# A blockwise triangular inversion whose updates take half of the columns

## Chip, cores and metric

The kernel runs on one core of a Trainium2 chip. The metric is the time of one execution on the device in microseconds (us): a median of runs. The profile is of one further execution.

## What is computed

One step of a decoder trunk with two layers: 2048 prompt tokens (four tiles of 512) and 8 sequences of 8 decode tokens, model width 1024. The first layer mixes tokens with a gated DeltaNet of six heads, the second with a short convolution; beside each runs a cross-attention into 256 memory tokens, and an output projection follows. What matters here is one step of the DeltaNet. For each head and each chunk of tokens a unit lower triangular system is solved:

```python
    decay = jnp.exp(jnp.where(tril, G[..., :, None] - G[..., None, :], -jnp.inf))
    kb = k * beta[..., None]
    A = jnp.tril(jnp.einsum('bnhid,bnhjd->bnhij', kb, k) * decay, -1)
    rhs = jnp.concatenate([kb * jnp.exp(G)[..., None], v * beta[..., None]], axis=-1)
    wu = lax.linalg.triangular_solve(A + jnp.eye(C, dtype=A.dtype), rhs, left_side=True,
                                     lower=True, unit_diagonal=True)
```

The kernel takes chunks of 128 tokens instead of 64 (the result is the same in exact arithmetic) and inverts the 128x128 matrix of each chunk. The decode tokens are one matrix of 64x64 with eight blocks of 8.

## The kernel before

**Order.** All engines follow one order that is fixed when the kernel is built. A planner (class Flow) runs generators as jobs with priorities and keeps a clock for each engine; each operation moves these clocks by a cost. The matmul helper mm prices a matmul of n fp16 columns at 3 + max(n, 64)/2.4 ns, an ACTIVATE from PSUM is priced at 52 ns + 0.83 ns for each element of a partition, and hops between engines have prices too. A job yields when it waits for another engine, and the planner then takes the job of the best priority that is ready by its clocks. The instructions come out in this order on every engine's queue, and on SP's for the DMAs.

**Work.** In the first layer a loop over heads and token tiles (head_tile) emits the projections of k, q, v and the gate: 24 fp16 matmuls of 512 columns each, weights and activations being split into a high and a low fp16 part. They fill PE while the jobs of the DeltaNet run beside them: wy_decay, wy_k, wy_q and wy_v prepare a head tile of four chunks, two jobs wy_inv invert its matrices (two chunks each), and scan goes through the chunks in order. There are 48 wy_inv for prompt tiles and 6 for the decode tile.

**The inversion** (wy_inv) keeps two fp16 matrices per chunk: U (upper triangular) and L (lower triangular, its transpose), both halves of one tile UL with four blocks of 128 columns: U of the two chunks, then L of the two chunks. Both hold the inverse of the diagonal blocks of the matrix, at first blocks of two. Level li = 1 to 6 goes from blocks of s = 2^li to blocks of 2s (1 to 2 in the decode tile):

1. PE: pq = A16^T L, one matmul of 128 columns per chunk.
2. DVE: qq = pq times a mask. The mask holds the scaled identity and the lower left quarter of each block of 2s, so qq is the identity plus the new quarter.
3. PE: pu = qq^T U and U^T qq, two matmuls of 128 columns per chunk, into four blocks of one PSUM bank.
4. ACT: one ACTIVATE copies the bank (512 columns, fp32) to the fp16 tile UL.

Step 1 of the next level reads L, step 3 reads U. After the last level one correction (tiles pe, ee, u1) follows, and scan waits for its result. The bank is a credit that is given back (gc_.put) after step 4, and qq's buffer (kqc.put) after step 3.

The profile names tiles without numbers: pu is the bank of step 3, ul the tile UL. All matmuls have line L330 (helper mm), all operations of ACT, DVE and POOL line L281 (the helper that keeps the clocks).

Of the kernel before, what the change touches and what calls it, by code (L numbers as in the profile page):

```python
# [15 lines left out]
AF = mybir.ActivationFunctionType  # L16
# [270 lines left out]
def hybrid_kernel(  # L287
# [26 lines left out]
    A = Eng(fl, "ACT", nc.scalar, in_psum)  # L314
# [4 lines left out]
    def mm(out, lhsT, rhs, start=True, stop=True):  # L319
        n = 1  # L320
        for s in rhs.shape[1:]:
            n *= s
        k = lhsT.shape[0]
        if rhs.dtype in (F16, BF16):
            c = 3.0 + max(n, 64) / (2.4 if k == P else 4.8)
        else:
            c = 10.0 + max(n, 128) / 0.6
        fl.op("PE", c if k == rows_in[0] else c + 100.0, out, (lhsT, rhs))
        rows_in[0] = k
        nc.tensor.matmul(out, lhsT=lhsT, rhs=rhs, start=start, stop=stop)  # L330
# [19 lines left out]
    def wait(*flags):  # L350
        for f in flags:
            if not f.on or f.t + HOP > fl.cur.t:
                yield f
# [33 lines left out]
    def psum(tag, shape, bufs, name):  # L387
        t = pp.tile(shape, F32, tag=tag, name=name, bufs=bufs)
        psum_names.add(t.tensor.name)
        return t  # L390
# [4 lines left out]
    def gbank(name):  # L395
        return psum("bank", [P, 4, P], 8, name)
# [10 lines left out]
    def k1(name, dt=F32):  # L407
        return gp.tile([P, 2, P], dt, tag="k1", name=name, bufs=NK1)
# [4 lines left out]
    def kq16(name):  # L413
        return gp.tile([P, 2, P], F16, tag="kq", name=name, bufs=NKQ)
# [985 lines left out]
    def rows(x, n, C):  # L1400
        return x[:n, :n].rearrange("p (o f) -> p o f", o=1).to_broadcast([n, C, n])
# [150 lines left out]
    def wy_inv(it, i):  # L1552

        n, hc = it.n, it.hc
        lv = 7 if n == P else 3
        yield from wait(it.M_ok[i])
        M = it.M[i]  # L1560
        G.tensor_tensor(M[:n, :hc, :n], M[:n, :hc, :n], rows(identKh, n, hc), op=ALU.add)
        yield
        yield from ulc.get()
        yield from kqc.get(2)
        A16 = kq16("A16")
        V.tensor_copy(A16[:n, :hc, :n], M[:n, :hc, :n])
        UL = gp.tile([P, 4, P], F16, tag="k1", name="ul", bufs=NK1)
        U, L = UL[:n, 0:2], UL[:n, 2:4]
        yield
        yield from gc_.get()  # L1570
        pq = gbank("pq")
        for z in range(hc):
            mm(pq[:n, z, :n], A16[:n, z, :n], identh[:n, :n])
        t = fl.cur.t
        G.tensor_tensor(U[:, :hc, :n], A16[:n, :hc, :n], rows(mask_u, n, hc), op=ALU.mult)
        fl.cur.t, fl.cur.eng = t, "PE"
        yield
        V.tensor_tensor(L[:, :hc, :n], pq[:n, :hc, :n], rows(masks[:, 0], n, hc), op=ALU.mult)
        gc_.put()
        yield  # L1580
        Ml = None
        for li in range(1, lv):
            yield from gc_.get()
            pq = gbank("pq")
            for z in range(hc):
                mm(pq[:n, z, :n], A16[:n, z, :n], L[:, z, :n])
            if Ml is None:
                t = fl.cur.t
                Ml = kq16("Ml")
                G.tensor_tensor(Ml[:n, :hc, :n], M[:n, :hc, :n], A16[:n, :hc, :n], op=ALU.subtract)  # L1590
                fl.cur.t, fl.cur.eng = t, "PE"
                Mc.put()
            yield
            yield from kqc.get()
            qq = kq16("qq")
            V.tensor_tensor(qq[:n, :hc, :n], pq[:n, :hc, :n], rows(masks[:, li], n, hc), op=ALU.mult)
            gc_.put()
            yield
            yield from gc_.get()
            pu = gbank("pu")  # L1600
            for z in range(hc):
                mm(pu[:n, z, :n], qq[:n, z, :n], U[:, z, :n])
            for z in range(hc):
                mm(pu[:n, 2 + z, :n], U[:, z, :n], qq[:n, z, :n])
            kqc.put()
            yield
            if hc == 2:
                A.activation(UL[:n, :, :n], pu[:n, :, :n], AF.Copy)
            else:
                A.activation(UL[:n, 0:4:2, :n], pu[:n, 0:4:2, :n], AF.Copy)  # L1610
            gc_.put()
            yield
        yield from gc_.get()
        pe = gbank("pe")
        for z in range(hc):
            mm(pe[:n, z, :n], A16[:n, z, :n], L[:, z, :n], start=True, stop=False)
            mm(pe[:n, z, :n], Ml[:n, z, :n], L[:, z, :n], start=False, stop=True)
        yield
        kqc.put(2)
        yield from kqc.get()  # L1620
        ee = kq16("ee")
        V.tensor_tensor(ee[:n, :hc, :n], rows(identKh, n, hc), pe[:n, :hc, :n], op=ALU.subtract)
        gc_.put()
        yield
        yield from uc.get()
        yield from gc_.get()
        pu = gbank("pu1")
        for z in range(hc):
            mm(pu[:n, z, :n], ee[:n, z, :n], U[:, z, :n])
        kqc.put()  # L1630
        yield
        it.u[i] = k1("u1")
        V.scalar_tensor_tensor(it.u[i][:n, :hc, :n], pu[:n, :hc, :n], 1.0 / MS, U[:, :hc, :n], op0=ALU.mult, op1=ALU.add)
        gc_.put()
        ulc.put()
        fl.set(it.u_ok[i])
# [170 lines left out]
    def head_tile(hd, t):  # L1807
# [13 lines left out]
        for i, (blk, w, dst) in enumerate(((6 + h, wk, kt_), (h, wq, qt_), (12 + h, wv, v_))):  # L1821
# [23 lines left out]
            if i == 0:  # L1845
                fl.spawn(3, chain(start, wy_decay(it)), "decay")
                fl.spawn(3, chain(start, wy_k(it, dn[0])), "wy_k")
                for z in range(it.nh):
                    fl.spawn(1, wy_inv(it, z), f"inv{z}")
            elif i == 1:  # L1850
                fl.spawn(3, chain(start, wy_q(it, dn[1])), "wy_q")
            else:
                fl.spawn(3, chain(start, wy_v(it, dn[2])), "wy_v")
# [449 lines left out]
```

## Time and profile before

| | us |
|---|---|
| median of 3 runs | 2224.36 |
| lowest, highest | 2221.85, 2230.78 |
| profiled execution | 2225.13 |
| its span (first to last instruction) | 2223.4 |
| from the first to the last update matmul of the inversion | 129.2 to 1050.6 |

The span is read as three parts. Up to about 130 us inputs are loaded and normed. Up to about 1056 us the first layer's projections run with the DeltaNet beside them. After that come the first layer's attention and output projection and then the second layer, in which nothing is inverted. Engines: PE is TensorE's matmul, PEld its weight load, DVE VectorE, ACT ScalarE, POOL GpSimd. The rows are in a section of their own below.

### The profile page before, as it was taken

The numbers are of one execution on the slowest core, as the hardware profiler recorded it, in microseconds if no ns is written. First come the engines' busy times: TensorE is split into PE (matmuls) and PEld (weight loads), VectorE is DVE, ScalarE is ACT, GpSimd is POOL, SyncE is SP. The second block draws the span as 40 slices with busy tenths as digits, with TensorE's granted clock in tenths as the row PEclk, the third lists the DMA queues.
The fourth block names the chain that finished last, engine by engine and source line by source line (L and its number), as shares of the span: only waits on it lengthen the run. The fifth ranks groups of instructions, "written<-read, shape, count | busy, mean of one in ns | idle before, by whom it ended". The sixth has DMA issues, their size and how long they took to land.

```text
span 2223.4 us, 43011 instructions
## 1 busy us (share of the span) xinstructions
PE 2147.2 (97%) x16176; PEld 1298.0 (58%) x16176; DVE 1488.9 (67%) x4228; ACT 1120.7 (50%) x2952; POOL 714.3 (32%) x901
## 2 busy tenths in 40 slices
PE   6889989999999999999999999999999999999998
PEld 5467657667666666666555454455444456555457
DVE  6988887887889878777777566355342437675354
ACT  5757665566657656566566345134221226653221
POOL 5655334442434433433222335012110212201322
PEclk9989999999999999999999999999999999999999
DMA  4201020201122102002134443022010111223433
GB/s 134 64 13 37 16 49 9 55 30 27 39 70 41 50 6 46 31 6 69 56 102 143 142 152 114 15 68 80 31 54 10 53 49 58 69 72 129 129 112 118
DMA packets 113634, 141.50 MB, mean 64 GB/s; under 512 B 50193, under 2 KB 67857, under 8 KB 113425
## 3 DMA queue, kind: packets, MB, share of 16 engines
q1 hardware_dynamic: 113424, 138.75, 20.5%
q8 instruction: 127, 2.08, 0.4%
q14 instruction: 83, 0.67, 0.1%
HBM read 99.22 MB, written 39.49 MB: 62 GB/s over the span
## 4 chain that ended last, share of the span: by engine, by line
PE 58%; DVE 3%; ACT 1%; issue 1%; DMA 1%; POOL 0%; POOLq 0%; DVEq 0%; ACTq 0%
PE psp L330 49%; PE psA L330 2%; PE psc L334 1%; PE pu L330 1%; PE po L330 1%; PE psc L330 1%; PE rb L330 1%; DVE wmx L281 1%; PE pq L330 1%; PE pqk L330 0%; DVE amx L281 0%; PE pkk L330 0%; DMA wraw<-in_wo 0%; DVE apT L281 0%; PE po L334 0%
## 5 line engine op out<-in xcount | busy, mean ns | idle before, releaser
L330 PE MATMUL psp<-ht,whl 128*128 128x512 f16 x5376 | 1270.0, 380 | 0.0
L330 PEld LDWEIGHTS <-whl 128*128 128x128 f16 x9408 | 753.6, 98 | 650.1 <-issue 12.6
L281 POOL TENSOR_TENSOR whl<-wraw,whl 128x512 f16<-128x512 f32 x184 | 216.8, 1182 | 448.0 <-ACT whl L281 400.2
L330 PE MATMUL psp<-hl,whl 128*128 128x512 f16 (+1 forms) x1728 | 342.4, 357 | 0.0
L281 ACT ACTIVATE ul<-pu 128x512 f16<-128x512 f32 x300 | 168.3, 582 | 79.6 <-PE pu L330 76.8
L281 ACT ACTIVATE wraw<-wraw,wsc 128x512 f32<-128x512 f32 (+1 forms) x186 | 131.7, 712 | 76.3 <-DVE wsc L281 44.6
L281 DVE SCALAR_TENSOR_TENSOR cacc<-psp,cws,cacc 128x511 f32<-128x511 f32 (+2 forms) x216 | 159.4, 738 | 10.1 <-ACT cacc L281 9.8
L281 POOL TENSOR_TENSOR nsq<-nsq 128x512 f32<-128x512 f32 (+2 forms) x105 | 100.6, 960 | 194.3 <-ACT nsq L281 149.1
L281 DVE TENSOR_TENSOR qq<-pq,masks 128x256 f16<-128x256 f32 x300 | 118.0, 407 | 51.1 <-PE pq L330 49.2
L281 DVE TENSOR_REDUCE wmx<-wraw 128x1 f32<-128x1024 f32 (+1 forms) x93 | 111.5, 1201 | 31.6 <-DMA wraw<-in_wb 24.5
L281 ACT ACTIVATE wg<-psp,hisc 128x512 f32<-128x512 f32 x64 | 44.0, 687 | 171.6 <-PE psp L330 171.4
L281 ACT ACTIVATE nsq<-xo 128x512 f32<-128x512 f32 (+1 forms) x72 | 41.4, 580 | 150.8 <-DVE xo L281 86.8
L281 ACT ACTIVATE whl<-wraw 128x512 f16<-128x512 f32 x184 | 114.8, 626 | 2.7
L281 DVE SCALAR_TENSOR_TENSOR xo<-psp,isc,xo 128x512 f32<-128x512 f32 (+1 forms) x72 | 49.6, 688 | 95.2 <-PE psp L330 95.2
L281 DVE SCALAR_TENSOR_TENSOR wg<-wg,psp 128x512 f32<-128x512 f32 x64 | 43.6, 681 | 87.8 <-ACT wg L281 87.8
L330 PEld LDWEIGHTS <-A 128*128 128x128 f16 x792 | 69.4, 100 | 41.1 <-issue 10.4
L281 ACT ACTIVATE ape<-psc,amx,sa 128x256 f32<-128x256 f32 x128 | 70.8, 561 | 31.7 <-DVE amx L281 31.6
L330 PE MATMUL pu<-ul,qq 128*128 128x128 f16 (+1 forms) x588 | 81.8, 224 | 3.9 <-DVE qq L281 3.1
L330 PE MATMUL pq<-ul,A 128*128 128x128 f16 (+1 forms) x588 | 77.0, 224 | 4.6 <-ACT ul L281 2.6
L330 PE MATMUL pu<-qq,ul 128*128 128x128 f16 (+1 forms) x588 | 81.2, 223 | 0.0
L281 POOL TENSOR_TENSOR rk<-sse,mhalf 128x4 f32<-128x4 f32 (+1 forms) x30 | 27.6, 919 | 159.9 <-DVE sse L281 118.8
L281 DVE SCALAR_TENSOR_TENSOR raw<-psp,wisc,cg 128x512 f32<-128x512 f32 x24 | 18.0, 749 | 86.9 <-PE psp L330 86.8
(344 smaller groups left out, 3641.0 us busy)
## 6 DMA issues: line engine op xcount, KB each, us to landing
br_sp<-wg SPq DMA_DIRECT2D x64, 256.0 KB, 2.0
brl<-br_sp SPq DMA_DIRECT2D x64, 256.0 KB, 2.9
wraw<-in_wb SPq DMA_DIRECT2D x28, 512.0 KB, 3.5
wraw<-in_wa SPq DMA_DIRECT2D x24, 512.0 KB, 3.5
xk<-in_x SPq DMA_DIRECT2D x64, 128.0 KB, 2.9
wraw<-in_wo SPq DMA_DIRECT2D x16, 512.0 KB, 3.4
xo<-in_x SPq DMA_DIRECT2D x32, 256.0 KB, 3.5
x_sp<-xo SPq DMA_DIRECT2D x32, 256.0 KB, 2.4
```

Source lines behind the costliest of these rows:

```text
L281: return f(out, *args, **kw)
L330: nc.tensor.matmul(out, lhsT=lhsT, rhs=rhs, start=start, stop=stop)
L334: nc.tensor.transpose(out, in_, ident)
```

## The change

In wy_inv, the update of each level (steps 3 and 4) takes half of the columns. A view splits the columns of U, L and qq into blocks of 2s and each block into a first and a second half of s columns. The matmuls for U take the second halves of U as the moving operand, those for L the first halves of qq: 64 columns each, in pieces of s columns, where it was 128 in one run. The results lie packed in PSUM, 64 columns for each matrix. Two ACTIVATEs instead of one copy them back, into the second halves of U and then into the first halves of L; the other halves keep what they had. The decode tile takes the same path with one chunk and 32 columns. Steps 1 and 2, the correction, and all other jobs are as before. The planner prices the new operations with the same formulas.

```diff
+        def halves(x, li):
+
+            v = x[:, :, :n].rearrange("p z (b h s) -> p z b h s", h=2, s=1 << li)
+            return v[:, :, :, 0], v[:, :, :, 1]
+
         for li in range(1, lv):
...
             yield from gc_.get()
-            pu = gbank("pu")
+
+            pu = gbank("pu").rearrange("p c (b s) -> p c b s", s=1 << li)
+            nb = n >> (li + 1)
+            first, second = halves(L, li), halves(U, li)
+            qf = halves(qq[:n], li)[0]
             for z in range(hc):
-                mm(pu[:n, z, :n], qq[:n, z, :n], U[:, z, :n])
+                mm(pu[:n, z, :nb], qq[:n, z, :n], second[1][:, z])
             for z in range(hc):
-                mm(pu[:n, 2 + z, :n], U[:, z, :n], qq[:n, z, :n])
+                mm(pu[:n, 2 + z, :nb], U[:, z, :n], qf[:, z])
             kqc.put()
             yield
-            if hc == 2:
-                A.activation(UL[:n, :, :n], pu[:n, :, :n], AF.Copy)
-            else:
-                A.activation(UL[:n, 0:4:2, :n], pu[:n, 0:4:2, :n], AF.Copy)
+            A.activation(second[1][:, :hc], pu[:n, :hc, :nb], AF.Copy)
+            A.activation(first[0][:, :hc], pu[:n, 2:2 + hc, :nb], AF.Copy)
             gc_.put()
             yield
```

## Rows read from the trace of the kernel before

**Rows 1.** The page: span, and each engine's busy time, share, instructions.

```profile
span 2223.4 us, 43011 instructions
PE 2147.2 (97%) x16176; PEld 1298.0 (58%) x16176; DVE 1488.9 (67%) x4228; ACT 1120.7 (50%) x2952; POOL 714.3 (32%) x901
```

**Rows 2.** The page: the chain that ended last, shares of the span by engine.

```profile
PE 58%; DVE 3%; ACT 1%; issue 1%; DMA 1%; POOL 0%; POOLq 0%; DVEq 0%; ACTq 0%
```

**Rows 3.** Stretches: start:end, length, busy us (count) PE PEld DVE ACT POOL, clock, DMA.

```profile
130.00:1056.00 926.00, 898.49 (x7495) 618.45 (x7494) 753.61 (x2430) 584.28 (x1780) 366.73 (x507) 0.99 0.14 36
...
1300.00:2224.00 924.00, 911.31 (x6261) 483.67 (x6259) 460.56 (x1092) 321.29 (x647) 206.89 (x226) 1.00 0.23 75
```

**Rows 4.** PE by shape: out<-in, count | busy us, mean ns | idle before.

```profile
L330 PE MATMUL pu<-ul,qq 128*128 128x128 f16 x576 | 79.2, 224 | 3.9 <-DVE qq L281 3.1
L330 PE MATMUL pu<-qq,ul 128*128 128x128 f16 x576 | 78.9, 224 | 0.0
```

**Rows 5.** Timeline of PE, 677.9 to 679.4: start, us, operation, count.

```profile
677.99 0.38 PE L330 MATMUL psA<-R,u 128*128 128x128 f32 x2
678.21 0.28 PE L330 MATMUL pu<-ul,qq 128*128 128x128 f16 x2
...
678.66 0.81 PE L330 MATMUL psp<-ht,whl 128*128 128x512 f16 x3
```

**Rows 6.** Timeline of PE in the attention, 1068 to 1070.

```profile
1068.58 0.51 PE L330 MATMUL po<-vt,apT 128*128 128x64 f16 x12
1068.93 1.24 PE L330 MATMUL psp<-ht,whl 128*128 128x512 f16 x5
```

**Rows 7.** Waits of PE, 130 to 1056: us in total, times, longest.

```profile
PE psA L330 <- ACT vh L281: 4.3, 1, 4.3
PE pu L330 <- DVE qq L281: 3.1, 6, 1.2
PE pq L330 <- ACT ul L281: 2.6, 5, 1.6
```

**Rows 8.** ACT by shape: count | busy us, mean ns | idle before.

```profile
L281 ACT ACTIVATE ul<-pu 128x512 f16<-128x512 f32 x288 | 165.6, 595 | 76.5 <-PE pu L330 73.7 <-PE psp L330 1.6
...
L281 ACT ACTIVATE kd<-pk 128x128 f32<-128x128 f32 x96 | 25.2, 282 | 3.6 <-PE pk L334 3.6
...
L281 ACT ACTIVATE raws<-psp,wisc 128x64 f32<-128x64 f32 x18 | 5.6, 319 | 0.9 <-PE psp L330 0.9
L281 ACT ACTIVATE wgs<-psp,hisc 128x64 f32<-128x64 f32 x16 | 5.1, 316 | 6.1 <-PE psp L330 5.4 <-PE pq L330 0.5 <-PE pam L330 0.2
```

**Rows 9.** Timeline of ACT, 500 to 506.5.

```profile
502.71 1.06 ACT L281 ACTIVATE ul<-pu 128x512 f16<-128x512 f32 x2
503.67 0.69 ACT L281 ACTIVATE wg<-psp,hisc 128x512 f32<-128x512 f32 x1
```

**Rows 10.** Timeline of ACT, 206.9 to 208.1.

```profile
206.97 0.26 ACT L281 ACTIVATE kd<-pk 128x128 f32<-128x128 f32 x1
207.13 0.19 ACT L281 ACTIVATION_READ_ACCUMULATOR kd<-pk 128x1 f32 x1
```

**Rows 11.** Timeline of all engines, 300 to 306: in brackets idle time before, releaser.

```profile
304.97 0.35 ACT L281 ACTIVATE caccs<-raws,cwa 128x64 f32<-128x64 f32 x1 [6.92 <-DMA raws<-in_gc]
305.28 0.37 ACT L281 ACTIVATE vh<-psA,bb 128x128 f32<-128x128 f32 x1
...
305.70 0.58 PE L330 MATMUL psA<-vh,kd 128*128 128x128 f32 x1 [4.26 <-ACT vh L281]
```

**Rows 12.** Shorter stretches, columns as in rows 3.

```profile
130.00:144.00 14.00, 10.98 (x117) 8.18 (x116) 11.93 (x37) 10.97 (x40) 8.29 (x12) 1.00 0.01 2
144.00:158.00 14.00, 13.15 (x116) 11.42 (x115) 6.80 (x27) 5.75 (x20) 6.31 (x9) 0.52 0.07 20
...
300.00:310.00 10.00, 5.74 (x30) 3.18 (x28) 5.54 (x16) 3.06 (x9) 2.31 (x3) 0.83 0.01 1
```

**Rows 13.** Operations on tile pu: count, ns min/median/max, first and last start.

```profile
L330 PE MATMUL pu<-ul,qq x588: 213/219/314, 129.2 to 1050.6; 128*128 128x128 f16 x192, 64*64 64x64 f16 x4
```

## What the change was predicted to do

> **What bounds the kernel now.** I read the page's engine table first: PE is busy for 97% of the span, DVE for 67% [rows 1]. The chain of work that ended last agrees: it runs mostly through PE [rows 2]. A busy PE is not yet a PE at its peak, so the next view is the table by stretches. The inversion lies only in the 926 us from 130 to 1056; there PE is busy for 898.5 us, DVE for 753.6 us (81%), ACT for 584.3 us (63%) [rows 3]. PE is thus idle for 926.0 - 898.5 = 27.5 us, 3%. From 1300 on there is no inversion and the change can only shift that part in time. So a matmul made shorter inside the first stretch should shorten the kernel nearly one for one, as long as the queue behind it is full; work taken off ACT should not show by itself.
>
> **The matmuls.** The update of a level is 4 matmuls (two chunks, U and L). There are 576 + 576 of them at 128 columns [rows 4]. Their mean of 224 ns is a latency: they overlap. What counts is the distance from start to start. In the timeline, four lines of two matmuls each begin at 678.21 us and the next operation begins at 678.66 [rows 5]: 0.45 us for 8, 56 ns each. The price of the same matmul at 64 columns is in the attention, where matmuls of 64 columns each have a weight load of their own too, as every matmul of this kernel has (16176 of both) [rows 1]. Twelve of them begin at 1068.58 and the next operation begins at 1068.93 [rows 6]: 0.35 us, 29 ns each. So each matmul gives back 27 ns, and 1152 x 27 ns = **31.1 us** on PE. The 24 small ones of the decode tile, at half the width, are worth under 0.5 us together and are left out.
>
> What of this is lost: where PE waits behind an update anyway, a shorter update only lengthens the wait. The waits that name the inversion's own tiles are small, 3.1 us for qq and 2.6 us for ul [rows 7], 11 waits in all, against 1152 matmuls. All idle time of PE in the stretch is 3%. I take a loss of twice that share, 6%, about 2 us, since slack is not spread evenly: **-29 us** remains.
>
> Here a rule of the Trainium skill speaks against the change. Rows 5 and 6 show 56 and 29 ns for pairs of weight load and matmul. The page TensorE: Matmul & The Clock Gate, section Back-to-back issue gap, holds that in a stream of such pairs both operations set the spacing, with about 81 ns at 128 columns. If the weight load were the limit, fewer columns would give nothing, the sum would be 0 and the time 2225; this trace disagrees with that figure by its 56 ns, and goes down to 29 ns.
>
> **The moving operand in pieces.** New is that the 64 columns are no longer one run: they are pieces of 2, 4, 8, 16, 32 and 64 fp16 elements in levels 1 to 6, with gaps as long between them. Both matmuls of the update read so (U's second halves, qq's first halves). No row here shows a moving fp16 operand in such pieces. From below, the bound is the 29 ns of rows 6; a gain beyond it is excluded, since as many columns stream. From above, the nearest slow rows are 56 ns (half rate, no gain, rows 5) and, farther, the fp32 matmuls just before in rows 5, two of 128 columns from 677.99 to 678.21, 110 ns each. I take 29 ns: the operands stay fp16 with 64 columns, as in rows 6, and only their addresses differ. If only the two levels with the shortest pieces (2 and 4) ran at half rate, a third of the gain would go: 10.4 us.
>
> The Trainium skill, Advanced Engine Details and Errata, section SBUF Cachelines, has lines of 16 bytes and asks for at least two hits on each. Pieces of 2 elements still give 4 of 8 elements of each line, so by that rule all six levels would run at full pace; no run here shows it yet.
>
> **The evacuation.** One ACTIVATE of 128x512 becomes two of 128x128 (two chunks by 64 columns). Rows 8 give 595 ns for the one and 282 ns for 128x128 from PSUM. Start to start, two of 128x512 take 0.96 us, 480 ns each [rows 9], and a 128x128 takes 160 ns before the next instruction starts [rows 10]. So ACT goes from 480 to 2 x 160 = 320 ns per update; 288 x 160 ns = 46 us come off ACT. That is off the path: ACT is at 63%. The new writes go to SBUF in pieces. ACT rows with 64 elements show 319 ns for a write in pieces of 8 (raws) and 316 ns for one run (wgs) [rows 8]; I cost the pieces at nothing, and the cover is ACT's slack. If the second instruction had to wait for the whole of the first, the pair would last 2 x 282 = 564 ns, still under 595.
>
> **The chain of a level.** pq, qq, pu, evacuation and again pq is serial. Matmuls give 4 x 27 = 108 ns and the evacuation 595 - (160 + 282) = 153 ns: 0.26 us per level, 1.6 us in six levels. The next pq waits for L alone, which is now the second of the two instructions, so that the 153 ns already counts both. Other strands and the projections cover this chain nearly everywhere; the most that it could give directly is the 5.7 us of rows 7. I count it at zero.
>
> **The order.** The order of all work is set ahead by a planner. The matmul helper prices 64 columns at 3 + 64/2.4 = 30 ns and ACT at 52 + 0.83 n, thus 2 x 158 against 477 ns. Both come close to the rows, so the planner's picture stays as true as it was. But it sorts all later jobs by these times, so the order on PE, ACT, DVE, POOL and on SP's queue may differ from the first update on. What such an order can cost is seen at 300 us: ACT has an instruction of the decode tile in front that waits 6.92 us for a DMA, and behind it stands the vh that PE needs; PE waits 4.26 us [rows 11]. The granted clock in that stretch of 10 us is 0.83: behind the wait PE ran for a while at 1.2 instead of 2.4 GHz. It was 0.52 in 144 to 158 us too, after a stretch in which PE was idle for 3 of 14 us [rows 12]. A new order can meet more or fewer of these. I cost that at zero, with both sides in the range: half clock in these two stretches cost 14 x 0.48 + 10 x 0.17 = 8.4 us, and with the 27.5 us of idle time 36 us are there to be won or added to. A change by about 40% of it is 14 us downward; upward I allow 20 us.
>
> **The sum.** The profiled execution took 2225.1 us, with a span of 2223.4; the median of the runs is 2224.4, so they are alike. 2225.1 - 29 = **2196 us**. The stages behind the inversion keep their length and begin earlier.
>
> **The rivals.** (1) A new order or a later clock takes most of the gain: 2225.1 - 29 + 20 = 2216 at the end of my allowance. For it: everything is ordered ahead, and one late DMA costs PE 4.3 us. Against it: waits that long are rare, one in 926 us [rows 7]. (2) The shortest pieces are read at half rate: 2196 + 10 = 2206. Nothing in the trace speaks for or against. (3) Weight loads or pieces hold all 64-column matmuls at 56 ns: 2225, no change. The 29 ns of rows 6 speak against the loads, not against the pieces. (4) Slower: reading in pieces costs more than half rate. The place is each of the 1152 updates; it decides from 56 + 11/1.152 = 66 ns per matmul, where the loss reaches 0.5% (11 us), and at the 110 ns of the fp32 rows the kernel would take 2225 + 1152 x 0.054 = 2287 us. (5) The shorter chain removes waits at the start and with them the low clock: 2196 - 14 = 2182. (6) That the change does not do what it says would show as an update that misses something. U is upper and L lower triangular, qq is the scaled identity plus the block below it, so that the other half of the columns is only multiplied by the identity; I give this no time of its own.
>
> **How the numbers follow.** About 0.5% (11 us) is what a measurement of this kernel can tell from no change. Forecast, 2188 to 2205: 0.66. Rival 5, down to 2182 or a little less: 0.07. Rival 2: 0.08. Rival 1, 2206 to 2216 and in the tail beyond: 0.10. Rival 3: 0.05. Rival 4: 0.04. The range of 2182 to 2216 takes in the forecast, rival 2, most of rivals 1 and 5, and leaves out some 0.15. Faster than 2213: 0.66 + 0.07 + 0.08 and a bit over half of rival 1, 0.87, less a little for orders that I can't see: 0.85. Within 0.5%: the rest of rival 1 and rival 3, 0.10. Slower: 0.05.
>
> **What would show it.** In the trace after: pu matmuls of 128x64, 1152 of them, at 29 ns from start to start in every level, with eight in 0.23 us where eight took 0.45. If levels 1 and 2 show 56 ns and the rest 29, rival 2 holds; if all do, rival 3. The ul evacuation should be 576 instructions of 128x128 at about 280 ns, with 160 ns between the two of a pair. The last pu, at 1050.6 us before [rows 13], should come some 29 us earlier, and the part from there to the end should keep its length of about 1173 us (2223.4 - 1050.6). If PE's idle time in the inversion's stretch grows by more than 10 us, or the granted clock there falls, rival 1 has set in. The prediction is wrong if the matmuls keep their 56 ns, or if they shrink and the stretch doesn't.

## The result

| | median, us | runs |
|---|---|---|
| before | 2223.88 (2221.85 to 2230.78) | 4 |
| after | 2193.22 (2190.70 to 2195.87) | 4 |

The ratio is 0.9857, with a 95% interval of 0.9832 to 0.9881: 31 us or 1.4% less. The profiled execution of after took 2192.52 us.

The page of after, its span and engines, and the mean granted clock, answer to [rows 1]:

```profile
span 2190.4 us, 43323 instructions
PE 2119.2 (97%) x16176; PEld 1268.8 (58%) x16176; DVE 1485.6 (68%) x4228; ACT 1083.4 (49%) x3252; POOL 717.6 (33%) x901
```

```profile
core 0: 2190.4 us, clock 0.989
```

PE loses 28 us of busy time, ACT 37 us. The number of matmuls is the same; 312 more instructions run, nearly all of them the second ACTIVATEs. The update matmuls by shape [rows 4] and on the timeline [rows 5]:

```profile
L330 PE MATMUL pu<-ul,qq 128*128 128x64 f16 x576 | 61.2, 196 | 4.3 <-DVE qq L281 3.3 <-DVE M L281 0.3
L330 PE MATMUL pu<-qq,ul 128*128 128x64 f16 x576 | 60.7, 195 | 0.0
```

```profile
496.29 0.22 PE L330 MATMUL pu<-ul,qq 128*128 128x64 f16 x2
496.34 0.22 PE L330 MATMUL pu<-qq,ul 128*128 128x64 f16 x2
496.40 0.22 PE L330 MATMUL pu<-ul,qq 128*128 128x64 f16 x2
496.46 0.22 PE L330 MATMUL pu<-qq,ul 128*128 128x64 f16 x2
496.52 0.81 PE L330 MATMUL psp<-ht,whl 128*128 128x512 f16 x3
```

Eight begin in 0.23 us, 29 ns each, as the attention's matmuls do in [rows 6]. The trace names the pieces that each matmul reads. Sorted by them, at full clock, the medians of the distance from start to start within an update are 29 to 30 ns with pieces of 2 and 4 elements and 29 ns in the other levels. The pieces cost next to nothing.

The evacuation by shape [rows 8], then on ACT's timeline [rows 9]:

```profile
L281 ACT ACTIVATE ul<-pu 128x128 f16<-128x128 f32 x576 | 122.5, 281 | 78.1 <-PE pu L330 73.9 <-PE pam L330 1.2 <-PE psp L330 0.8
```

```profile
503.78 0.77 ACT L281 ACTIVATE ul<-pu 128x128 f16<-128x128 f32 x4
504.41 0.41 ACT L281 ACTIVATE dd<-pd 128x256 f32<-128x256 f32 x1
```

Four of them take 0.63 us to the next start, 158 ns each. Last, PE's waits from 130 us to the end of the inversion [rows 7], the stretch itself [rows 3] and the last update [rows 13]:

```profile
PE psA L330 <- DVE qs L281: 3.8, 6, 1.8
PE pq L330 <- DVE A L281: 3.4, 5, 1.7
PE pu L330 <- DVE qq L281: 3.3, 8, 0.9
...
PE pq L330 <- ACT ul L281: 1.5, 3, 0.8
```

```profile
130.00:1012.60 882.60, 858.71 (x7397) 582.13 (x7396) 745.51 (x2412) 540.40 (x2061) 365.46 (x503) 0.98 0.14 36
```

```profile
L330 PE MATMUL pu<-ul,qq x588: 189/193/261, 128.6 to 1012.2; 128*128 128x64 f16 x192, 64*64 64x32 f16 x4
```

PE is idle for 882.6 - 858.7 = 23.9 us here. The longest wait of before, 4.3 us behind a late DMA [rows 11], is not there any more; the longest is now 1.8 us. The last update comes 38 us earlier, not 29, and what follows it has become 5 us longer (1178 instead of 1173 us). That does not fit 1152 matmuls that each give 27 ns and nothing else, and it is what the experiments were made for.

**An account in three terms.** For every profile below I split the span into PE's idle time (span less PE's busy time), the low clock ((1 - mean granted clock) x span: what half clock cost in time; the printed clock is exact to about 1 us) and the rest, which is work at full clock. Before: 76.2 + 24.5 + 2122.7. After: 71.2 + 24.1 + 2095.1. So -27.6 us of the -33.0 are PE's work, and -5.4 are waits and clock.

### The profile page after: what moved, and what is told of

Its sections match the earlier page's. It is cut to its first block, busy times and chain, and to the rows that moved or that the text cites. A ratio compares the mean times of both kernels' runs of the same rounds, so it can differ in the third digit from the quotient of the medians.

```text
span 2190.4 us, 43323 instructions
## 1 busy us (share of the span) xinstructions
PE 2119.2 (97%) x16176; PEld 1268.8 (58%) x16176; DVE 1485.6 (68%) x4228; ACT 1083.4 (49%) x3252; POOL 717.6 (33%) x901
## 4 chain that ended last, share of the span: by engine, by line
PE 80%; DVE 14%; ACT 2%; POOL 2%; issue 2%; DMA 1%; SPq 0%; POOLq 0%; DVEq 0%; ACTq 0%
PE psp L330 62%; PE psA L330 4%; DVE cacc L281 3%; PE pu L330 2%; PE pq L330 2%; PE rb L330 2%; PE psc L334 1%; DVE nhs L281 1%; PE psc L330 1%; PE po L330 1%; DVE qq L281 1%; DVE wmx L281 1%; PE pqk L330 1%; PE pkk L330 1%; PE psS L330 1%
## 5 line engine op out<-in xcount | busy, mean ns | idle before, releaser
L281 ACT ACTIVATE ul<-pu 128x128 f16<-128x128 f32 x600 | 125.8, 278 | 82.1 <-PE pu L330 77.8
L281 POOL TENSOR_TENSOR rk<-sse,mhalf 128x4 f32<-128x4 f32 (+1 forms) x30 | 27.6, 919 | 149.3 <-DVE sse L281 103.5
L281 ACT ACTIVATE cacc<-psp,cws 128x512 f32<-128x512 f32 x72 | 49.8, 691 | 42.0 <-PE psp L330 35.9
L330 PEld LDWEIGHTS <-qq 128*128 128x128 f16 (+1 forms) x588 | 49.9, 101 | 33.0 <-DVE qq L281 10.6
```

The lines of the kernel that those rows point to most:

```text
L281: return f(out, *args, **kw)
```

## The experiments

Times are medians, each against runs of the kernel before on the same chip (2223.9 to 2225.4 us). Span, idle time, low clock and work are those of the one profiled execution, which is not always close to the median: for the operations of before in the order of after it took 2221.1 us (the longest of ten), for one ACTIVATE in the order of after 2188.8 us (the shortest of five).

| kernel | us | ratio, 95% interval | span | idle | low clock | work |
|---|---|---|---|---|---|---|
| before | 2223.9 | | 2223.4 | 76.2 | 24.5 | 2122.7 |
| evacuation alone | 2223.5 | 0.9995, 0.9980 to 1.0009 | 2223.7 | 75.1 | 24.5 | 2124.1 |
| operations of before, order of after | 2214.6 | 0.9959, 0.9944 to 0.9973 | 2219.0 | 69.3 | 26.6 | 2123.1 |
| before, EXTRA 33 | 2216.0 | 0.9962, 0.9949 to 0.9975 | 2214.2 | 70.7 | 17.7 | 2125.8 |
| before, EXTRA 27 | 2239.8 | 1.0072, 1.0060 to 1.0084 | 2236.1 | 84.0 | 29.1 | 2123.0 |
| after | 2193.2 | 0.9857, 0.9832 to 0.9881 | 2190.4 | 71.2 | 24.1 | 2095.1 |
| after, EXTRA 33 | 2197.0 | 0.9878, 0.9863 to 0.9892 | 2194.5 | 75.6 | 24.1 | 2094.8 |
| after, EXTRA 27 | 2194.6 | 0.9875, 0.9859 to 0.9891 | 2192.9 | 73.6 | 26.3 | 2093.0 |
| operations of after, order of before | 2207.0 | 0.9920, 0.9901 to 0.9938 | 2206.9 | 79.6 | 30.9 | 2096.4 |
| matmuls alone | 2205.5 | 0.9909, 0.9890 to 0.9928 | 2204.0 | 80.4 | 30.9 | 2092.7 |
| one ACTIVATE | 2210.3 | 0.9934, 0.9918 to 0.9950 | 2208.3 | 83.6 | 33.1 | 2091.6 |
| one ACTIVATE, order of after | 2196.0 | 0.9877, 0.9859 to 0.9896 | 2186.6 | 71.2 | 19.7 | 2095.7 |
| pq halved too | 2209.1 | 0.9927, 0.9911 to 0.9943 | 2204.6 | 90.7 | 35.3 | 2078.6 |
| pq halved, one ACTIVATE | 2201.7 | 0.9900, 0.9883 to 0.9916 | 2202.9 | 88.2 | 37.4 | 2077.3 |

The last column falls into three groups, whatever the order: 2122.7 to 2125.8 us where the updates have 128 columns (mean 2123.7), 2091.6 to 2096.4 where they have 64 (mean 2094.2), about 2078 where pq has 64 too. The two in the middle, idle time and low clock, move by tens of us between kernels of the same operations.

### The evacuation alone

```diff
-                A.activation(UL[:n, :, :n], pu[:n, :, :n], AF.Copy)
...
+            A.activation(halves(U, li)[1][:, :hc], halves(pu[:n, 0:2], li)[1][:, :hc], AF.Copy)
+            A.activation(halves(L, li)[0][:, :hc], halves(pu[:n, 2:4], li)[0][:, :hc], AF.Copy)
```

> The matmuls of the update keep all 128 columns; only the evacuation is halved: two ACTIVATEs of 128x128 that read the changed halves out of the full PSUM blocks. Theory (the gain is PE's issue time of 1152 matmuls, 27 ns each): no change, 2224 us within 6. Rival (the gain comes through the shorter chain and the time taken off ACT): 0.15 of the 0.26 us per level are the evacuation's, so more than half of the 31 us should appear, about 2206 us. ACT's evacuations fall from 288 x 595 ns to 576 x about 280 ns under both.

Measured 2223.5 us: no change. ACT did get shorter, from 1120.7 us [rows 1] to 1082.3, and the chain of a level with it:

```profile
L281 ACT ACTIVATE ul<-pu 128x128 f16<-128x128 f32 x576 | 123.1, 281 | 86.0 <-PE pu L330 83.7 <-PE pq L330 0.8 <-POOL ba L281 0.5
```

ACT's evacuations now wait longer for pu (83.7 instead of 73.7 us): what ACT saves turns into waiting for PE. The rival with the chain falls, as far as one order can tell.

### The matmuls alone

```diff
             A.activation(second[1][:, :hc], pu[:n, :hc, :nb], AF.Copy)
             A.activation(first[0][:, :hc], pu[:n, 2:2 + hc, :nb], AF.Copy)
+            A.activation(first[0][:, :hc], pu[:n, 2:2 + hc, :nb], AF.Copy)
```

> The matmuls are halved as in the change, and the evacuation is made as long as before: a third ACTIVATE of 128x128 repeats the second one (3 x 158 = 474 ns of ACT beside 477 before, and the last one ends 0.59 us after the first began). Theory (PE's issue time): the whole gain stays, 2193 us within 6. Rival (chain and ACT): only the matmuls' share of the chain stays, 0.11 of 0.26 us, about 2211 us.

Measured 2205.5 us, between the two. By itself it is inconclusive, since this kernel has an order of its own, planned for three ACTIVATEs. The account says where the difference from after lies: the work is the same (2092.7 against 2095.1), idle time is 9 us and low clock 7 us more. Of the idle time, waits of PE that name the evacuation are 3.0 us in the inversion's stretch here and 1.5 us in after, so the repeated ACTIVATE holds PE up directly for little of the 12 us. That the order accounts for all the rest is not shown.

### New operations in the old order, old operations in the new one

In both kernels the planner is told other prices than the operations have; apart from the changed operations, the queues of all five engines then match those of before and of after instruction by instruction.

```diff
# operations of after, order of before
-                mm(pu[:n, z, :nb], qq[:n, z, :n], second[1][:, z])
+                mm(pu[:n, z, :nb], qq[:n, z, :n], second[1][:, z], priced=n)
...
+            A.activation(second[1][:, :hc], pu[:n, :hc, :nb], AF.Copy, priced=52.0 + 0.83 * 2 * hc * n)
+            A.activation(first[0][:, :hc], pu[:n, 2:2 + hc, :nb], AF.Copy, priced=0.0)
# operations of before, order of after
+                mm(pu[:n, z, :n], qq[:n, z, :n], U[:, z, :n], priced=n // 2)
...
+                A.activation(UL[:n, :, :n], pu[:n, :, :n], AF.Copy, priced=2 * (52.0 + 0.83 * n))
```

> The instructions of the change, but the planner is told the prices of before (128 columns for each update matmul, 477 ns for the pair of ACTIVATEs), so that every queue has the order of the kernel before. Theory (PE's issue time): the gain is there without the new order, 2193 us within 6. Rival (the new order gives the gain or a good part of it): 2224, or for a part as large as half, 2208. The shift of the inversion's end by 38 us with a tail longer by 5 us, seen in the trace after the change, should go: with the old order the last update matmul should come 29 to 31 us earlier than 1050.6 and the tail stay at 1173 us.

> The instructions of before, but the planner is told the prices of the change, so that every queue has the order of the kernel after. Theory (PE's issue time): 2224 us within 6. Rival (order): 2193, or 2208 for half. If both this and the run with the old order lie off by the same few us to opposite sides, that is what the order is worth.

Measured 2207.0 and 2214.6 us. My theory missed both: the operations without the new order give 18 us (2224.97 to 2207.04), the order without the operations 10. So the operations alone, in these two orders, are worth 18 and about 21 us (2214.6 to 2193.2), and the order of after about 10 to 14.

With the same order, the profiles can be laid side by side: the k-th matmul of one is the k-th of the other, 16176 pairs. I summed the changes of the distance to the next matmul:

| | before to new operations in its order | old operations in the order of after, to after |
|---|---|---|
| after an update matmul | -29.9 | -30.8 |
| PE idle behind it, in one of the two | +4.0 | +2.8 |
| granted clock differs | +4.9 | -1.9 |
| all others | +4.3 | +1.2 |
| sum, us | -16.6 | -28.6 |

So the updates give their 30 us in either order, and in the order of before 13 come back between these profiles. The second column makes the order of after look better than it is, since its first profile is of the execution of 2221.1 us: by the medians only 21.4 us remain of 30.8. By the span and granted clock listed for every execution, the low clock costs on average 22.7 us before and 29.8 us with the new operations in its order, 19.5 us with the old operations in the order of after and 24.1 us after. In both orders, then, about 5 to 7 us come back as low clock and about 5 us as waits and small delays.

One place in the order of before shows how. The timeline of PE in the order of before, first with the operations of before, then with those of after:

```profile
1023.28 0.60 PE L330 MATMUL psp<-hs_t,whl 128*128 128x64 f16 x15
1024.52 0.42 PE L330 MATMUL psp<-hs_t,whl 128*128 128x64 f16 x9 [0.64 <-issue]
```

```profile
1004.12 0.48 PE L331 MATMUL psp<-hs_t,whl 128*128 128x64 f16 x11
1006.40 0.85 PE L331 MATMUL psp<-hs_t,whl 128*128 128x64 f16 x13 [1.79 <-issue]
```

PE stands still 1.15 us longer in the second, for nothing that the profile names. The 10 us around it, in the same sequence (the clock is the third number from the right):

```profile
1021.00:1031.00 10.00, 8.14 (x97) 5.21 (x94) 7.23 (x26) 7.59 (x19) 1.61 (x2) 1.00 0.07 29
```

```profile
1004.00:1014.00 10.00, 8.21 (x67) 4.76 (x68) 5.71 (x22) 5.24 (x16) 1.48 (x2) 0.66 0.07 27
```

The granted clock falls at 1005.5 us, inside the longer wait, and PE gets 1.2 GHz for much of these 10 us, where it had 2.4 GHz throughout. That is 10 x 0.34 = 3.4 us of low clock; some 3 us of it fall behind the wait and cost more than the 1.15 us by which the wait is longer.

The expectation for the inversion's end held by half. The last update, here with the new operations in the order of before and then with the old ones in the order of after:

```profile
L331 PE MATMUL pu<-ul,qq x588: 189/193/261, 129.1 to 1034.1; 128*128 128x64 f16 x192, 64*64 64x32 f16 x4
```

```profile
L331 PE MATMUL pu<-ul,qq x588: 213/219/314, 130.3 to 1040.1; 128*128 128x128 f16 x192, 64*64 64x64 f16 x4
```

In the order of before it comes 16.5 us earlier, not 29 to 31, but what follows keeps its 1173 us. With the old operations in the order of after the tail is 1179 us long, so the longer tail of after belongs to its order.

### Other orders

One constant of the planner is changed, before and after. The operations and their prices stay.

```diff
-EXTRA = 30.0
+EXTRA = 33.0   # and 27.0
```

> The kernel before, the planner's one constant EXTRA (its extra hop between engines) 33 instead of 30 ns: the same instructions in another order of the same kind. Theory (the order of the kernel after was worth some 10 us by luck, orders of one kind scatter by that much): anywhere from 2212 to 2234, and no nearer to the kernel before than that. Rival (an order made with the right prices is about as good as any other, so that only the new operations' order is better): 2224 within 4.

> The kernel after, EXTRA 33 instead of 30 ns. Theory (the operations are worth about 20 us, orders scatter by about 10): 2205 within 10, so likely slower than the kernel after with its 2193. Rival (an order made for the shorter operations keeps all of their 31 us): 2193 within 4.

> The kernel before, EXTRA 27 instead of 30 ns. As for 33: by the theory anywhere from 2212 to 2234, by the rival 2224 within 4.

> The kernel after, EXTRA 27 instead of 30 ns. As for 33: by the theory 2205 within 10, by the rival 2193 within 4. With the pairs measured so far there are then two orders told apart from the operations in each kernel: if the mean of the kernels after lies 18 to 23 us below the mean of the kernels before, the loss between PE's 31 us and the gain is real; if it lies about 30 below, the pair with the order of before was the exception.

Measured 2216.0 and 2197.0 (33), 2239.8 and 2194.6 (27). The kernel before does scatter, over 24 us with 2223.9 in between, and 2239.8 lies outside even the 2212 to 2234 that the theory allowed. The three kernels after lie within 4 us. The difference is 19, 45 and 31 us in the three pairs, 32 in the mean, and 27 with the two crossed pairs (18 and 21). By the rule set for the last of these runs, a mean near 30 would make the pair in the order of before the exception; but with 24 us of scatter among the kernels before, three pairs cannot tell 20 from 30. The four numbers fit neither theory whole: the scatter of before speaks for the first, the closeness of the three afters for the second. That an order planned for the right prices keeps the whole gain is not shown either: the two kernels with halved updates and other evacuations, planned with their own prices, came out at 2205.5 and 2210.3.

### Further along the same way

The mask keeps only first-half columns of pq and the identity, so pq can be halved too; DVE then copies the identity's columns into qq.

```diff
-                mm(pq[:n, z, :n], A16[:n, z, :n], L[:, z, :n])
+                mm(pqv[:n, z, :nb], A16[:n, z, :n], halves(L, li)[0][:, z])
...
-            V.tensor_tensor(qq[:n, :hc, :n], pq[:n, :hc, :n], rows(masks[:, li], n, hc), op=ALU.mult)
+            qf, qs_ = [x[:, :hc] for x in halves(qq[:n], li)]
+            V.tensor_copy(qs_, halves(rows(identh, n, hc), li)[1])
+            V.tensor_tensor(qf, pqv[:n, :hc, :nb], halves(rows(masks[:, li], n, hc), li)[0], op=ALU.mult)
```

> The kernel after, with the first matmul of each level halved too: pq takes only the first halves of L's columns (64 instead of 128), since the mask keeps nothing of the other half but the identity; DVE writes the identity's columns into qq by a copy (128x128 fp16) and masks only the 128x128 that were computed. Theory (columns on PE count): 576 matmuls x 27 ns = 15.5 us less on PE, with an order of its own that scatters by about 10: 2178 within 10. Rival (the 31 us of the update were all that the inversion's matmuls could give, since other engines now end the waits): 2193 or above; DVE gets one more instruction per level, 288 in all.

Measured 2209.1 us: slower than after by 16. The work fell as expected, by 16 us (2094.2 to 2078.6), and idle time and low clock ate twice that. PE's row names what it waits for, and the row of the copy and the timeline of DVE, POOL and PE show a part of the cause:

```profile
L330 PE MATMUL pu<-ul,qq 128*128 128x64 f16 x576 | 62.0, 198 | 20.4 <-DVE qq L281 19.2 <-DVE sse L281 0.6
```

```profile
L281 DVE COPY qq<-identh x300: 154/185/2546, 126.9 to 1024.4; 128x128 f16<-128x128 f16 x145, 64x32 f16<-64x32 f16 x5
```

```profile
620.68 2.55 DVE L281 COPY qq<-identh 128x128 f16<-128x128 f16 x1
620.78 0.66 POOL L281 TENSOR_TENSOR Ml<-M,A 128x256 f16<-128x256 f32 x1
...
621.40 0.66 POOL L281 TENSOR_TENSOR ul<-A,mask_u 128x256 f16<-128x256 f16 x1
622.03 1.15 POOL L281 TENSOR_TENSOR whl<-wraw,whl 128x512 f16<-128x512 f32 x1
623.13 0.67 POOL L281 TENSOR_TENSOR Ml<-M,A 128x256 f16<-128x256 f32 x1
623.15 0.28 DVE L281 TENSOR_TENSOR qq<-pq,masks 128x128 f16<-128x128 f32 x1
...
623.48 0.23 PE L330 MATMUL pu<-ul,qq 128*128 128x64 f16 x2 [2.38 <-DVE qq L281]
```

The copy's median is 185 ns, but one lasts 2546 ns while POOL runs one instruction after another, and PE waits 2.38 us for the mask behind it. 52 of the 300 copies take over 300 ns, 25 us more than their median in sum. POOL is busy beside each of these 52 for at least 85% of its length, and none of the 195 copies that begin while POOL is idle is among them; yet 38 copies ran beside POOL for over 90% of their length and stayed short. The Trainium skill, Advanced Engine Details and Errata, section GPSIMD Details, says that POOL shares a read and a write interface with DVE and conflicts with DVE instructions in a 2-port performance mode or with two SBUF inputs. The rows fit that if the copy, which has one input, runs in such a mode; no row shows whether it does.

The long copies are not the whole of it. Of the 19.2 us that PE waits for qq, 6.4 us (7 waits) come behind copies of 337 to 2546 ns; two waits at 143 and 149 us, 8.5 us together, come behind copies of 302 and 181 ns. How much of the loss is the copy's and how much the order's stays open: this kernel was not run in the order of after, and a copy that doesn't use DVE was not run either.

One ACTIVATE for all four halves, packed side by side in PSUM:

```diff
...
-            A.activation(second[1][:, :hc], pu[:n, :hc, :nb], AF.Copy)
-            A.activation(first[0][:, :hc], pu[:n, 2:2 + hc, :nb], AF.Copy)
+            if hc == 2:
+                o = bass.AP(tensor=UL.tensor, offset=UL.offset + sz,
+                            ap=[list(UL.ap[0]), [2 * P - sz, 2], [2 * sz, 2 * nb], [1, sz]])
+                A.activation(o, pu[:n], AF.Copy)
...
```

> The kernel after, with one ACTIVATE of 128x256 in place of the two of 128x128 (the four changed halves packed side by side in PSUM and written by one address pattern). ACT is about 52 ns shorter per update (one 264 ns instead of two of 158), 15 us in all, and the chain by about 50 ns per level. Theory (PE is the bound, ACT is covered): 2193 within 6. Rival (ACT's chain ends the waits): 2180.

> Both of these: halved pq and one ACTIVATE. Theory: as with the halved pq, 2178 within 10. Rival with the chain: below 2170.

Measured 2210.3 us with the one ACTIVATE and 2201.7 us with both. Both theories missed, and so did both rivals: less is done on ACT, and on PE too in the second, and yet they are 17 and 8 us slower than after. With the one ACTIVATE the work was that of after (2091.6 against 2095.1), idle time was 12 and low clock 9 us more. Two causes were left, the order or the instruction itself, and the last run keeps the order of after:

> The single ACTIVATE of 128x256 once more, but the planner is told the price of the two (316 ns), so that every queue keeps the order of the kernel after. Theory (ACT is covered, and the 17 us that the single ACTIVATE lost against the kernel after came from its order alone): 2193 within 5, PE's idle time and low clock as in the kernel after. Rival (one instruction that writes U and L at once makes both wait for more, and costs by itself): 2205 to 2212 also with this order.

Measured 2196.0 us, within the expectation. Page and clock of the two kernels with one ACTIVATE, in its own order and then in that of after:

```profile
PE 2124.7 (96%) x16176; PEld 1275.0 (58%) x16176; DVE 1499.3 (68%) x4228; ACT 1067.4 (48%) x2964; POOL 716.2 (32%) x901
```

```profile
core 0: 2208.3 us, clock 0.985
```

```profile
PE 2115.4 (97%) x16176; PEld 1267.6 (58%) x16176; DVE 1484.1 (68%) x4228; ACT 1067.2 (49%) x2964; POOL 717.3 (33%) x901
```

```profile
core 0: 2186.6 us, clock 0.991
```

ACT has the same 1067 us in both. PE's idle time is 83.6 in the one and 71.2 us in the other, to the tenth that of after. The ACTIVATE is neither a loss nor a gain that can be told from the measurement; the 14 us between the two are order. No kernel here is faster than after.

## Why the prediction was right, step by step

**The time.** 2196 was forecast, 2193.2 measured, inside 2182 to 2216, and faster as expected.

**The matmuls** were sized right: 29 ns at 64 columns in all levels, 29.9 and 30.8 us from the pairs of equal order, -29.5 us of work between the means of the five and the seven kernels with 128 and 64 columns, against 31.1. Rivals 2, 3 and 4 (pieces read slowly, weight loads as the limit, slower than half rate) fall with the same rows. Rival 6 had no time of its own: the rows show that all updates and evacuations ran, not what they computed. Rival 5, a time near 2182, was not met. The signs set for rival 1 were not met either: PE's idle time in the inversion's stretch fell from 27.5 to 23.9 us, and the granted clock there stayed (0.9853 before, 0.9845 after, which print as 0.99 and 0.98). More on the order below.

**What is lost** was the weak step. I took 2 us, from the share of idle time in the stretch, as though idle time would stay as it is. With the order held fixed it grew: in the order of before, 13 of 30 us came back, 4 as idle time, 5 as low clock, 4 as small delays. The reason given (slack behind an update makes the wait longer) is right in kind for the idle time and says nothing of the low clock, and the size was too small by a factor of six there. In the order of after the profiles suggest that it was near right (28.6 of 30.8 us stay), but by the medians 9 of 31 us come back there too, so that it was too small by a factor of four to five.

**The order at zero** was not zero either, and it hid the loss: the order of after is better than that of before by about 10 us also with the old operations (2214.6). This is of the size by which orders of before differ among themselves (2216.0 to 2239.8). Along either way from before to after, -30 + 13 - 14 or -10 - 31 + 9, the loss and the order nearly cancel. The price of -14 to +20 us that I allowed for this was of the right size: over the twelve kernels with 128 or 64 columns in the update and pq as before, idle time and low clock together lie between 88 and 117 us, against 101 before. So the range was sound and the point was partly luck.

**The evacuation** off the path: right, shown by the last run, which keeps the order of after, and supported by the run with the evacuation alone. ACT's busy time fell by 37 us, where 46 us from start to start had been forecast, and nothing hung on it. **The chain** at zero: no run speaks against it.

**What would show it:** the last update was to come 29 us earlier with an unchanged tail. It came 38 us earlier with a tail 5 us longer. This was the sign in the first profile that something else had moved.

Open: whether orders planned for the shorter operations are better as a rule. Three say so (2193 to 2197), two do not (2205.5, 2210.3).

## What to carry to other kernels

When all queues follow one order fixed ahead, a change has two parts, the operation and the new order; build the operation into the old order, and the old operation into the new one, before believing either. Split a span into idle time, low clock and work: here the work of each kernel lay within 3 us of the mean of those with the same matmul columns, while the other two together moved by nearly 30 us between kernels of the same or nearly the same operations. A better operation that comes out slower (one ACTIVATE instead of two) may only have drawn a worse order. And before a profile is read as the kernel, compare its execution with the median: here one that was 6.5 us longer hid most of a loss.

## What was not expected of the hardware

Moving fp16 operands in pieces of 2 elements with gaps of 2 run at 29 to 30 ns per 64 columns, one run of 64 at 29. Where PE waited 1.8 us instead of 0.6, the granted clock was 0.66 over the 10 us around and behind the wait; the same sequence had 1.00. A DVE copy from fp16 to fp16 with a median of 185 ns lasted up to 2546 ns beside POOL.
